# Hybrid RWKV-7 and dilated-attention layer: the second head's operands of the recurrent chain shifted by one 64-block, its diagonal results kept by one VectorE operation

## The chip, the cores and the metric

The kernel runs on one core of one Trainium2 chip. The metric is the device time of one execution in microseconds, the median of three runs for the kernel before. The engines are named as in the profile: PE is TensorE's matmul, PEld its weight load, DVE is VectorE, ACT is ScalarE, POOL is GpSimd, SP issues most transfers. Each engine works its instructions off in the order in which the program lists them, and waits at the first one that isn't ready.

## The reference, cut to what matters

One decoder layer on x of shape (1, 1024, 1024) in float32. An RMSNorm and one input projection give the inputs of two branches: 16 heads of RWKV-7 time mixing and 16 heads of dilated window attention. Both are gated and projected out together, with a final RMSNorm. The change lies in the time mixing, whose core is a recurrence over 1024 tokens with a 64 by 64 state per head:

```
def step(state, inp):
    r_t, w_t, k_t, v_t, av_t, bv_t = inp
    sa = jnp.einsum('bhvk,bhk->bhv', state, av_t)
    state = (state * w_t[:, :, None, :] + sa[..., None] * bv_t[:, :, None, :]
             + v_t[..., None] * k_t[:, :, None, :])
    return state, jnp.einsum('bhvk,bhk->bhv', state, r_t)
xs = (r_h, w_h, k_h, v_h, -kk, kk * a_h)   # w_h = exp(-exp(w)), kk a normalised key
_, y = lax.scan(step, s0, xs)
```

## The kernel before, in words

The time mixing is computed in chunks of 64 tokens. A unit is two heads (a pair, on partitions 0 to 63 and 64 to 127) and one half of the sequence, that is 8 chunks; 8 pairs by 2 halves give 16 units, worked off one after the other. While one unit is in the recurrent chain, the next is being inverted (`late`, `invert`), the one after that prepared (`prepare`, `products`), and the one before finished (`finish`). The loop in `rwkv` (line 346 on) writes these into 24 slots per unit, and after each slot takes some matmuls of the input projection from a generator (`advance`, line 363; L179 in the profile, each 128x512). They are there for PE to work on while the chain waits. The final order on each engine is set by the framework's scheduler, which reorders what is written by its own estimates of costs; so the order changes in many places when a few operations change.

The chain (`chain`, line 684) has three steps per chunk, each a matmul whose result goes from PSUM through one "spread" back to SBUF, where the next matmul takes it as its moving operand:

- `first`: z from the state Sd and the operand array AR (z<-Sd), spread into zd; and into T the products with Vd and Sd (T<-Vd, T<-Sd).
- `second`: z from zd and the inverse U (z<-zd), spread with the scale rn into ud.
- `third`: T from ud and TU (T<-ud), spread with the decay dec into the next Sd. The next chunk's z<-Vd follows.

The two heads are computed in one matmul. zd, ud and Sd are block diagonal, [128, 2, 64], with zeros in the off-diagonal blocks; the heads' results come out on partitions 0 to 63, one head in columns 0 to 63, the other in 64 to 127. `spread` therefore moves head 0's 64x64 block on DVE (L704 for zd, L707 for ud and Sd) and head 1's on ACT (L705, L708), which also changes its partitions:

```
if scale is None:
    V.tensor_copy(out=out[er[0], 0], in_=q[0:64, 0:64])
    S.copy(out=out[er[1], 1], in_=q[0:64, 64:128])
else:
    V.tensor_scalar(out=out[er[0], 0], in0=q[0:64, 0:64], scalar1=scale[0], ...)
    S.activation(out=out[er[1], 1], in_=q[0:64, 64:128], func=AF.Copy, scale=scale[1])
```

Other lines that are named below: L413 forms the log decays lw, L422 sums them, L438 and L170 are ACT work of the preparation and of the projection's weights, L483 is the receptance written into AR, L569 and L570 copy and mask products into MV, L604 and L606 are the columns of the inversion (two small DVE operations each), L627 and L655 transpose U, L216 is the token shift on DVE. After the time mixing (from about 840 us) come the attention and the output projection, which the change doesn't touch.

Of the kernel before, what the change touches and what calls it, by code (L numbers as in the profile page):

```python
# [24 lines left out]
C = 64  # L25
# [20 lines left out]
class Kern:  # L46
# [237 lines left out]
    def rwkv(self, pairs=range(NPAIR), apairs=range(NPAIR)):  # L284
        nc = self.nc
        with ExitStack() as ctx:
# [21 lines left out]
            for a in self.ARs:  # L308
                nc.gpsimd.memset(a[:, NC_ * 192:], 0.0)
                a = self.c192(a)  # L310
                for e in range(2):
                    er = slice(e * 64, e * 64 + 64)
                    nc.gpsimd.tensor_copy(out=a[er, :, 0], in_=bc(self.ident[er, er].unsqueeze(1), (64, NC_, 64)))
            self.d0 = pers.tile([128, 2, C + 1], F32, name="d0")
# [71 lines left out]
    def prepare(self, d):  # L386
# [78 lines left out]

# [28 lines left out]
    def late(self, d):  # L494
# [28 lines left out]
        def keys2(c4):  # L523
            tq, cs = t["tq"], slice(c4 * 4, c4 * 4 + 4)
            for e in range(2):
                er = slice(e * 64, e * 64 + 64)
                S.copy(out=d["TU"][er, cs, 0], in_=tq[0:64, :, e])
                S.copy(out=self.c192(d["MV"])[er, cs, 0], in_=tq[64:128, :, e])

# [13 lines left out]
    def products(self, d):  # L543
        nc = self.nc
        V, S, G = nc.vector, nc.scalar, nc.gpsimd
        er = [slice(0, 64), slice(64, 128)]

        def step(c4):
            AR, BK = d["AR"], d["BK"]
            if c4 == 0:  # L550
                d["TU"] = self.lng.tile([128, NC_, 3, 64], F32, name="TU")
                d["MV"] = self.lng.tile([128, NC_ * 192 + 2], F32, name="MV")
                G.memset(d["MV"][:, NC_ * 192:], 0.0)
            cs = slice(c4 * 4, c4 * 4 + 4)
            q = [self.ps_a.tile([128, 4, 128], F32, name=f"pa{e}") for e in range(2)]
            for b in range(4):
                c = c4 * 4 + b
                for e in range(2):
                    nc.tensor.matmul(q[e][:, b], lhsT=BK[er[e], c], rhs=AR[er[e], c * 192 + 64:c * 192 + 192], start=True,  # L559
                                     stop=True)  # L560
            d["pq"] = q

        def step2(c4):
            cs, q = slice(c4 * 4, c4 * 4 + 4), d["pq"]
            for e in (1, 0):
                V.tensor_tensor(out=d["TU"][er[e], cs, 1:3].rearrange("p c a t -> p c (a t)"), in0=q[e][0:64],
                                in1=bc(self.mask[0:64, 1].unsqueeze(1), (64, 4, 128)), op=ALU.mult)
                f = self.c192(d["MV"])[er[e], cs, 1:3].rearrange("p c a t -> p c (a t)")
# [21 lines left out]
    def invert(self, d, U):  # L590
# [17 lines left out]
        def clear():  # L608
            G.memset(U[:, 0:NC_], 0.0)

        def back():
            ud = self.dpool.tile([4, 16, 16, 16], F32, name="ud")
            nc.sync.dma_start(out=ud.rearrange("b q s t -> (b q) (s t)"), in_=d["UB"])
            for e in range(2):
                for b in range(4):
                    r = e * 64 + b * 16
                    nc.sync.dma_start(out=U[r:r + 16, 0:NC_, b * 16:b * 16 + 16],
                                      in_=ud[b, 8 * e:8 * e + 8].rearrange("q s t -> s q t"))
# [5 lines left out]
        def m0():  # L624
            t["UT"] = self.tmp("vr2", "UT", (128, NC_, C))
            t["Xs"] = self.inv.tile([128, NC_, 32], F32, name="Xs")
            V.transpose(out=fl(t["UT"]), in_=fl(U[:, 0:NC_]))  # L627

        def m1():
            xq = t["xq"] = self.ps_tr.tile([128, NC_, 16], F32, name="xq", tag="tr")  # L630
            for c in range(NC_):
                for g in range(4):
                    b = 32 * (g % 2)
                    nc.tensor.matmul(xq[hs(g), c], lhsT=t["LT"][rs(g), c, b:b + 16], rhs=U[rs(g), c, b + 16:b + 32], start=True,
                                     stop=True, skip_group_check=True)
# [5 lines left out]
        def m2():  # L641
            dq = t["dq"] = self.ps_tr.tile([128, NC_, 16], F32, name="dq", tag="tr")
            for c in range(NC_):
                for g in range(4):
                    b = 32 * (g % 2)
                    nc.tensor.matmul(dq[hs(g), c], lhsT=t["UT"][hs(g), c, b:b + 16], rhs=t["Xs"][hs(g), c, 0:16], start=True,
                                     stop=True, skip_group_check=True)

        def m2c():
            for g in range(4):  # L650
                b = 32 * (g % 2)
                S.copy(out=U[hs(g), 0:NC_, b + 16:b + 32], in_=t["dq"][hs(g)])
# [87 lines left out]
    def heads_out(self, d, c4):  # L740
# [423 lines left out]
```

## Time and profile before

| what | value |
|---|---|
| median of 3 runs | 1553.68 us (1553.39 to 1553.86) |
| profiled execution's own time | 1555.3 us |
| its span, first to last instruction | 1553.6 us |
| busy share of the span: PE, PEld, DVE, ACT, POOL | 96%, 77%, 65%, 58%, 28% |
| mean granted TensorE clock | 0.998 of full speed |
| chain that ended last, by engine | PE 60%, DVE 17%, ACT 16%, issue 3%, DMA 2%, POOL 1% |

A busy PE is not a PE at its peak, since its matmuls overlap and their ends are modelled. What a change on another engine can be worth to a kernel like this is read from where PE waits, and for what.

### The profile page before, as it was taken

How to read it: one execution, taken by the hardware profiler on the slowest of the kernel's cores; microseconds unless marked ns; L12 is line 12 of the kernel's file. 1: busy time of each engine (PE TensorE's matmuls, PEld its weight loads, DVE VectorE, ACT ScalarE, POOL GpSimd, SP SyncE). 2: the span in 40 equal slices, each digit the busy share in tenths (PEclk: the TensorE clock that was granted, in tenths of full speed). 3: DMA queues.
4: the chain of work that ended last, by engine and by line, in shares of the span. 5: the costliest groups of instructions: out<-in, count | busy, mean ns of one | idle time of the engine just before them, and what ended most of it. 6: DMA issues, size and time to landing. Idle time of an engine off the chain costs nothing.

```text
span 1553.6 us, 29135 instructions
## 1 busy us (share of the span) xinstructions
PE 1486.1 (96%) x10721; PEld 1201.3 (77%) x10721; DVE 1009.3 (65%) x2776; ACT 897.6 (58%) x2080; POOL 442.0 (28%) x563
## 2 busy tenths in 40 slices
PE   5999999999999999999999999999999999899997
PEld 4877777777777777777777788888888888787886
DVE  6866776667776677766743557667676666956144
ACT  6655666666676666666643556555565565655221
POOL 3211111111111121112211534334443343456442
PEclk9999999999999999999999999999999999999999
DMA  6321111111111111111111201111111111426452
GB/s 199 90 48 33 41 40 39 41 34 40 47 32 41 47 33 41 39 38 41 34 39 34 70 28 42 35 35 34 38 52 34 36 55 55 159 92 203 142 161 99
DMA packets 178829, 94.87 MB, mean 61 GB/s; under 512 B 58413, under 2 KB 164606, under 8 KB 178686
## 3 DMA queue, kind: packets, MB, share of 16 engines
q1 hardware_dynamic: 174942, 86.19, 19.4%
q10 hardware_dynamic: 3744, 6.82, 1.3%
q8 instruction: 84, 1.38, 0.4%
q14 instruction: 59, 0.48, 0.1%
HBM read 75.01 MB, written 17.83 MB: 60 GB/s over the span
## 4 chain that ended last, share of the span: by engine, by line
PE 60%; DVE 17%; ACT 16%; issue 3%; DMA 2%; POOL 1%; SPq 0%; DVEq 0%; ACTq 0%; POOLq 0%
PE pq L179 28%; PE oq L1048 10%; PE o L994 3%; PE z L693 3%; PE T L693 3%; PE mp L921 2%; PE sp L954 2%; ACT Y L745 1%; DVE I L422 1%; ACT MV L569 1%; PE sp L974 1%; ACT Vd L513 1%; DVE TB L604 1%; ACT shtmp L213 1%; PE pa L559 1%
## 5 line engine op out<-in xcount | busy, mean ns | idle before, releaser
L179 PE MATMUL pq<-xh,wh 128*128 128x512 f32 x1040 | 429.1, 413 | 0.0
L179 PE MATMUL pq<-xl,wh 128*128 128x512 f32 x1040 | 412.3, 396 | 0.0
L179 PE MATMUL pq<-xh,wl 128*128 128x512 f32 x1040 | 303.3, 409 | 0.0
L179 PEld LDWEIGHTS pq<-xh,wh 128*128 128x128 f32 x1040 | 195.9, 188 | 32.6 <-ACT xh L157 0.3
L179 PEld LDWEIGHTS pq<-xl,wh 128*128 128x128 f32 x1040 | 196.4, 189 | 30.9 <-DVE xl L158 0.4
L179 PEld LDWEIGHTS pq<-xh,wl 128*128 128x128 f32 x1040 | 184.5, 189 | 31.9
L1048 PE MATMUL oq<-ow,qr 128*128 128x512 f32 x512 | 161.9, 394 | 1.2 <-ACT ow L1029 0.6
L982 POOL TENSOR_TENSOR pl<-p,ph 128x512 fp32r<-128x512 f32 (+2 forms) x96 | 102.3, 1072 | 202.2 <-ACT ph L981 182.4
L923 DVE CUSTOM_DVE_ANT_0 mp<-mp,maskq 128x512 f32<-128x512 f32 (+1 forms) x192 | 105.5, 570 | 68.4 <-PE mp L921 59.9
L977 ACT ACTIVATE p<-p 128x512 f32<-128x512 f32 (+2 forms) x144 | 64.6, 452 | 104.2 <-DVE p L976 103.3
L171 POOL TENSOR_TENSOR wl<-wraw,wh 128x512 fp32r<-128x512 f32 x64 | 85.5, 1354 | 110.4 <-PE pq L179 58.4
L1043 POOL TENSOR_TENSOR vr<-kr,qr 128x512 fp32r<-128x512 f32 (+2 forms) x68 | 90.8, 1340 | 80.5 <-ACT qr L1042 70.0
L1048 PEld LDWEIGHTS oq<-ow,qr 128*128 128x128 f32 x512 | 95.9, 188 | 22.8 <-ACT ow L1029 1.1
L1048 PE MATMUL oq<-ow,vr 128*128 128x512 f32 x256 | 101.2, 395 | 1.9 <-POOL vr L1043 1.9
L170 ACT CAST wh<-wraw 128x512 fp32r<-128x512 f32 x138 | 80.7, 616 | 28.6 <-PE pq L179 23.4
L1042 ACT CAST qr<-kr 128x512 fp32r<-128x512 f32 (+2 forms) x68 | 40.2, 594 | 93.5 <-PE oq L1048 52.0
L976 DVE TENSOR_TENSOR p<-sp,maskt 128x512 f32<-128x512 f32 (+2 forms) x144 | 65.2, 457 | 43.3 <-PE sp L974 41.9
L570 POOL TENSOR_SCALAR_AFFINE_SELECT MV<-MV 64x512 f32<-64x512 f32 x64 | 47.8, 747 | 125.2 <-ACT MV L569 114.2
L708 ACT ACTIVATE ud<-z,rn 64x64 f32<-64x64 f32 x128 | 39.3, 307 | 65.3 <-DVE ud L707 63.6
L707 DVE TENSOR_SCALAR ud<-z,rn 64x64 f32<-64x64 f32 x128 | 34.3, 268 | 58.1 <-PE z L693 57.9
L693 PEld LDWEIGHTS T<-ud,TU 128*128 128x128 f32 x256 | 42.5, 188 | 34.8 <-ACT ud L708 28.2
L708 ACT ACTIVATE Sd<-T,dec 64x64 f32<-64x64 f32 x120 | 36.9, 307 | 53.5 <-DVE Sd L707 52.0
(236 smaller groups left out, 3158.4 us busy)
## 6 DMA issues: line engine op xcount, KB each, us to landing
wraw<-in_w_in_dram SPq DMA_DIRECT2D x138, 256.0 KB
kr<-mixd SPq DMA_DIRECT2D x60, 256.0 KB
oraw<-in_w_out_dram SPq DMA_DIRECT2D x16, 512.0 KB
xt<-in_x_dram SPq DMA_DIRECT2D x8, 512.0 KB
ld<-TU SPq DMA_DIRECT2D x32, 128.0 KB
mixd<-zt SPq DMA_DIRECT2D x16, 256.0 KB
mixd<-gt SPq DMA_DIRECT2D x16, 256.0 KB
xr<-in_x_dram ACTq DMA_DIRECT2D x16, 256.0 KB
```

Source lines behind the costliest of these rows:

```text
L170: nc.scalar.copy(out=wh[:, ks], in_=raw)
L171: eng.tensor_tensor(out=wl[:, ks], in0=raw, in1=wh[:, ks].bitcast(F32), op=ALU.subtract)
L179: return [lambda i=i, a=a, b=b: self.nc.tensor.matmul(q, lhsT=a, rhs=b, start=(i == 0), stop=(i == len(ops) - 1)) for i, (a, b) in enumera ...
L570: G.affine_select(out=f, in_=f, pattern=[[0, 4], [-1, 2], [1, 64]], compare_op=ALU.is_ge, fill=0.0, base=0, channel_multiplier=-1)
L693: mm = lambda out, w, x, start, stop: nc.tensor.matmul(out, lhsT=w, rhs=f2(x), start=start, stop=stop, skip_group_check=True)
L708: S.activation(out=out[er[1], 1], in_=q[0:64, 64:128], func=AF.Copy, scale=scale[1])
L923: V.tensor_tensor_reduce(out=mp[:, :kn], in0=mp[:, :kn], in1=self.maskq[:, v0:v0 + kn], op0=ALU.add, op1=ALU.max, scale=1.0, scalar=-3e38, ...
L976: V.tensor_tensor(out=p[:, :qn], in0=sp[:, :qn], in1=self.maskt[:, u0:u0 + qn], op=ALU.add)
L977: S.activation(out=p[:, :qn], in_=p[:, :qn], func=AF.Exp)
L982: G.tensor_tensor(out=pl[:, :qn], in0=p[:, :qn], in1=ph[:, :qn].bitcast(F32), op=ALU.subtract)
L1043: nc.gpsimd.tensor_tensor(out=ml, in0=raw, in1=mh.bitcast(F32), op=ALU.subtract)
L1048: nc.tensor.matmul(q, lhsT=m[:, i], rhs=v, start=(k == 0 and j == 0), stop=(k == 15 and j == 2))
```

## The change

Head 1's operands are laid one 64-block later than head 0's, so that the matmuls put head 0's result on partitions 0 to 63 and head 1's on 64 to 127, where the spread needs it. A full 128x128 result then has the wanted blocks on its diagonal, and unwanted products off it. For ud and Sd one scalar_tensor_tensor on DVE scales the whole 128x128 and multiplies it with the constant block mask `bd`; ACT has no part in it. For zd the result is not shifted (both heads on partitions 0 to 63), and both halves are copied by DVE. Along with this:

- the operands AR, TU, MV and U change their layout: the identity block, receptance and masks go to other blocks for head 1 (`ra`), U's head 1 starts one block later, and `second` loads 128 columns of U as weights instead of 66;
- the receptance (L483) becomes two operations of 64 partitions, the mask on POOL (L570) two operations of half the size, the transposes of U and its clearing 576 columns instead of 512;
- the log decays move from DVE to ACT; the small ACT copies rn1 and dec's second half go.

```
 def logs():
-    V.tensor_scalar(out=lw[:, :, 0:C], in0=c3(th), scalar1=-DECAY / 2, scalar2=-DECAY / 2,
-                    op0=ALU.mult, op1=ALU.add)
+    S.activation(out=lw[:, :, 0:C], in_=c3(th), func=AF.Copy, scale=-DECAY / 2, bias=-DECAY / 2)
...
 def decrease():
-    d["dec"] = self.mid.tile([64, 2, NC_], F32, name="dec", bufs=3)
-    G.tensor_copy(out=d["dec"][:, 0], in_=Ux[0:64, :, 0])
-    S.copy(out=d["dec"][:, 1], in_=Ux[64:128, :, 0])
+    d["dec"] = self.mid.tile([128, NC_], F32, name="dec", bufs=3)
+    G.tensor_copy(out=d["dec"], in_=Ux[:, :, 0])
...
-    d["rn1"] = self.mid.tile([64, NC_], F32, name="rn1", bufs=3)
-    S.copy(out=d["rn1"], in_=rn[64:128])
...
 def receptance():
-    V.tensor_tensor(out=self.c192(d["AR"])[:, :, 1], in0=c3(d["rs"]), in1=d["W"][:, :, 1:C + 1], op=ALU.mult)
+    for e in range(2):
+        er = slice(e * 64, e * 64 + 64)
+        V.tensor_tensor(out=self.c192(d["AR"])[er, :, 1 - e], in0=c3(d["rs"])[er], in1=d["W"][er, :, 1:C + 1],
+                        op=ALU.mult)
...
 def step2(c4):
-        S.copy(out=f, in_=q[e][64:128])
-        G.affine_select(out=f, in_=f, pattern=[[0, 4], [-1, 2], [1, 64]], compare_op=ALU.is_ge, fill=0.0, base=0,
-                        channel_multiplier=-1)
+        S.copy(out=f, in_=cat(q[e][64:128]))
+        for j in range(2):
+            G.affine_select(out=f[:, :, j], in_=f[:, :, j], pattern=[[0, 4], [1, 64]], compare_op=ALU.is_ge, fill=0.0,
+                            base=-j, channel_multiplier=-1)
...
 def m0():
-    V.transpose(out=fl(t["UT"]), in_=fl(U[:, 0:NC_]))
+    V.transpose(out=fl(t["UT"]), in_=fl(U))
...
 def spread(out, q, scale):
-    if scale is None:
-        V.tensor_copy(out=out[er[0], 0], in_=q[0:64, 0:64])
-        S.copy(out=out[er[1], 1], in_=q[0:64, 64:128])
-    else:
-        V.tensor_scalar(out=out[er[0], 0], in0=q[0:64, 0:64], scalar1=scale[0], scalar2=None, op0=ALU.mult)
-        S.activation(out=out[er[1], 1], in_=q[0:64, 64:128], func=AF.Copy, scale=scale[1])
+    V.scalar_tensor_tensor(out=f2(out), in0=q, scalar=scale, in1=self.bd, op0=ALU.mult, op1=ALU.mult)
...
 def first(c):
-    spread(zd, t["z"][:, 0], None)
+    V.tensor_copy(out=zd[er[0], 0], in_=t["z"][0:64, 0, 0:64])
+    V.tensor_copy(out=zd[er[1], 1], in_=t["z"][0:64, 0, 64:128])
...
 def second(c):
-    mm(t["z"][0:66, 1], f2(d["U"])[:, c * 64:c * 64 + 66], self.zds[c % 2], True, True)
-    spread(self.uds[c % 2], t["z"][:, 1], [d["rn"][0:64, c:c + 1], d["rn1"][:, c:c + 1]])
+    mm(t["z"][:, 1], f2(d["U"])[:, c * 64:c * 64 + 128], self.zds[c % 2], True, True)
+    spread(self.uds[c % 2], t["z"][:, 1], d["rn"][:, c:c + 1])
...
 def third(c):
-    spread(self.Sds[(c + 1) % 2], T, [dec[:, e, n:n + 1] for e in range(2)])
+    spread(self.Sds[(c + 1) % 2], T, dec[:, n:n + 1])
```

The order on the engines moves with it. The place shown is the second chunk of the unit that runs at 510 us in the trace of before, around the spread into ud. In these rows zd, ud and Sd are the chain's spreads, TB and UB the inversion's columns, AR, BK and ks the preparation, bv, rs and wl other work. DVE before:

```order
L704 COPY zd_127<-z 64x64
L606 TENSOR_TENSOR UB<-UB,TB 64x12x4
L469 SCALAR_TENSOR_TENSOR AR_143<-ks,prm,W 128x8x64
L604 TENSOR_TENSOR TB<-UB,AB 64x39
L472 SCALAR_TENSOR_TENSOR BK<-ta,Ux 128x8x64
L606 TENSOR_TENSOR UB<-UB,TB 64x13x3
L476 SCALAR_TENSOR_TENSOR BK<-ks,prm,BK 128x8x64
L604 TENSOR_TENSOR TB<-UB,AB 64x28
L707 TENSOR_SCALAR ud_129<-z,rn 64x64
```

DVE now, at the same place:

```order
L717 COPY zd_127<-z 64x64
L607 TENSOR_TENSOR TB<-UB,AB 64x48
L718 COPY zd_127<-z 64x64
L609 TENSOR_TENSOR UB<-UB,TB 64x12x4
L421 SCALAR_TENSOR_TENSOR I<-d_154,lw 128x130
L607 TENSOR_TENSOR TB<-UB,AB 64x39
L609 TENSOR_TENSOR UB<-UB,TB 64x13x3
L607 TENSOR_TENSOR TB<-UB,AB 64x28
L609 TENSOR_TENSOR UB<-UB,TB 64x14x2
L607 TENSOR_TENSOR TB<-UB,AB 64x15
L609 TENSOR_TENSOR UB<-UB,TB 64x15
L707 SCALAR_TENSOR_TENSOR ud_129<-z,rn,bd 128x128
```

The three long operations of the preparation (AR, BK, BK) no longer stand between zd and ud; they come after ud. The two copies into zd have another operation between them, as 47 of the 128 such pairs have.

ACT before, from the preparation's L438 on (a), with the two casts of weights (wh) around the spread into ud:

```order
L438 ACTIVATE a<-ta,hk 128x512
L170 CAST wh<-wraw 128x512
L708 ACTIVATE ud_129<-z,rn_4899 64x64
L170 CAST wh<-wraw 128x512
L708 ACTIVATE Sd_122<-T_5937,dec 64x64
L213 ACTIVATE shtmp<-pq,prm 128x512
L705 COPY zd_126<-z 64x64
L708 ACTIVATE ud_128<-z,rn_4899 64x64
```

ACT now, at the same place:

```order
L432 ACTIVATE Ux<-I 128x520
L170 CAST wh<-wraw 128x512
L436 ACTIVATE a<-ta,hk 128x512
L170 CAST wh<-wraw 128x512
L213 ACTIVATE shtmp<-pq,prm 128x512
L745 COPY Y<-T_5833 64x256 x2
```

The spreads are gone from ACT, and nothing of the chain stands behind its long operations.

PE before, from z<-zd to the next chunk's z<-Sd (pq is the projection, bq the bonus product):

```order
L693 MATMUL z<-zd_127,U_118 66x128
L179 MATMUL pq<-xh_79,wl 128x512 x4
L533 MATMUL bq<-bh,bdr 128x512
L533 MATMUL bq<-bl,bdr 128x512
L179 MATMUL pq<-xh_79,wl 128x512 x2
L693 MATMUL T_5937<-ud_129,TU 128x128
L693 MATMUL z<-Vd_120,MV 66x128
L179 MATMUL pq<-xh_79,wl 128x512 x2
L693 MATMUL T_6206<-Vd_120,MV 128x128
L179 MATMUL pq<-xh_78,wh 128x512
L693 MATMUL z<-Sd_122,AR_144 66x128
```

PE now, over the same steps:

```order
L697 MATMUL z<-zd_127,U_118 128x128
L179 MATMUL pq<-xh_79,wl 128x512 x4
L697 MATMUL T_5833<-ud_129,TU 128x128
L697 MATMUL z<-Vd_120,MV 66x128
L532 MATMUL bq<-bh,bdr 128x512
L532 MATMUL bq<-bl,bdr 128x512
L179 MATMUL pq<-xh_79,wl 128x512 x4
L697 MATMUL z<-Sd_122,AR_144 66x128
```

Between z<-zd and T<-ud stood eight wide matmuls, now four; the other four moved behind T<-ud, where six now stand ahead of z<-Sd instead of three.

## Rows read from the trace of the kernel before

**Rows 1.** Windows: the time-mixing stretch; busy us and (instructions) of each engine, clock, DMA.

```profile
80.00:840.00 760.00, 729.76 (x7042) 567.62 (x7041) 514.26 (x1676) 476.87 (x1239) 124.91 (x242) 1.00 0.16 39
```

**Rows 2.** Waits of PE: who waited for whom; us in total, times, longest.

```profile
PE T L693 <- ACT ud L708: 8.9, 15, 1.3
PE z L693 <- ACT zd L705: 4.8, 15, 0.5
PE bq L533 <- ACT Vd L513: 4.5, 8, 1.5
PE z L693 <- ACT Sd L708: 3.8, 19, 0.5
```

**Rows 3.** Waits of PE's weight loads, same columns.

```profile
PEld T L693 <- ACT ud L708: 28.2, 56, 1.8
PEld z L693 <- ACT Sd L708: 24.3, 48, 0.9
PEld z L693 <- ACT zd L705: 14.8, 26, 0.9
```

**Rows 4.** Groups by line and shape, the chain on PE: count, busy us, mean ns, idle before.

```profile
L693 PE MATMUL T<-ud,TU 128*128 128x128 f32 x256 | 55.4, 298 | 10.0 <-ACT ud L708 8.9
L693 PE MATMUL z<-Sd,AR 128*66 128x128 f32 x256 | 51.4, 282 | 4.8 <-ACT Sd L708 3.8
L693 PE MATMUL z<-zd,U 128*66 128x128 f32 x256 | 50.4, 278 | 4.9 <-ACT zd L705 4.8
L693 PE MATMUL T<-Vd,MV 128*128 128x128 f32 x256 | 49.6, 275 | 0.0
...
L693 PE MATMUL z<-Vd,MV 128*66 128x128 f32 x256 | 49.0, 273 | 0.0
...
L693 PEld LDWEIGHTS T<-ud,TU 128*128 128x128 f32 x256 | 42.5, 188 | 34.8 <-ACT ud L708 28.2
...
L693 PEld LDWEIGHTS z<-zd,U 128*66 128x66 f32 x256 | 32.5, 137 | 27.8 <-ACT zd L705 14.8
```

**Rows 5.** Timeline of PE at 508.5 us: start, us, instruction, [idle before].

```profile
508.60 0.38 PE L693 MATMUL z<-zd,U 128*66 128x128 f32 x2
...
511.94 0.49 PE L693 MATMUL T<-ud,TU 128*128 128x128 f32 x2 [0.69 <-ACT ud L708]
```

**Rows 6.** Timeline of DVE at the same place.

```profile
510.13 0.27 DVE L707 TENSOR_SCALAR ud<-z,rn 64x64 f32<-64x64 f32 x1
```

**Rows 7.** Timeline of ACT at the same place.

```profile
510.23 0.82 ACT L438 ACTIVATE a<-ta,hk 128x512 f32<-128x512 f32 x1
510.95 0.60 ACT L170 CAST wh<-wraw 128x512 fp32r<-128x512 f32 x1
511.58 0.31 ACT L708 ACTIVATE ud<-z,rn 64x64 f32<-64x64 f32 x1
```

**Rows 8.** Groups by line and shape: DVE operations that price the new ones.

```profile
L707 DVE TENSOR_SCALAR ud<-z,rn 64x64 f32<-64x64 f32 x128 | 34.3, 268 | 58.1 <-PE z L693 57.9
...
L704 DVE COPY zd<-z 64x64 f32<-64x64 f32 x128 | 27.0, 211 | 40.5 <-PE z L693 38.7
...
L976 DVE TENSOR_TENSOR p<-sp,maskt 128x512 f32<-128x512 f32 x32 | 22.0, 688 | 31.4 <-PE sp L974 31.4
...
L976 DVE TENSOR_TENSOR p<-sp,maskt 128x128 f32<-128x128 f32 x48 | 13.1, 274 | 6.6 <-PE sp L974 5.5 <-POOL pl L982 0.9
...
L216 DVE SCALAR_TENSOR_TENSOR rs<-pq,om,shtmp 128x512 f32<-128x512 f32 x16 | 12.0, 750 | 0.7
```

**Rows 9.** Groups by line on DVE between 200 and 700 us: the log decays.

```profile
L413 DVE TENSOR_SCALAR lw<-th 128x512 f32<-128x512 f32 x11 | 4.7, 425 | 0.6
```

**Rows 10.** Windows: 5 us in the unit's first half, columns as in rows 1.

```profile
499.00:504.00 5.00, 4.51 (x29) 3.63 (x28) 4.83 (x18) 3.08 (x10) 0.53 (x2) 1.00 0.00 0
```

**Rows 11.** Groups by line and shape: the mask on POOL.

```profile
L570 POOL TENSOR_SCALAR_AFFINE_SELECT MV<-MV 64x512 f32<-64x512 f32 x64 | 47.8, 747 | 125.2 <-ACT MV L569 114.2 <-DVE vs L216 5.0 <-DVE ks L216 4.0
```

**Rows 12.** Waits of DVE for POOL.

```profile
DVE vs L216 <- POOL MV L570: 5.7, 7, 0.9
```

More of the change, by code (lines that the diff above doesn't have):

```diff
@@ L312, in rwkv @@
                     er = slice(e * 64, e * 64 + 64)
-                    nc.gpsimd.tensor_copy(out=a[er, :, 0], in_=bc(self.ident[er, er].unsqueeze(1), (64, NC_, 64)))
+                    nc.gpsimd.tensor_copy(out=a[er, :, e], in_=bc(self.ident[er, er].unsqueeze(1), (64, NC_, 64)))
             self.d0 = pers.tile([128, 2, C + 1], F32, name="d0")
@@ L526, in keys2 @@
                 er = slice(e * 64, e * 64 + 64)
-                S.copy(out=d["TU"][er, cs, 0], in_=tq[0:64, :, e])
-                S.copy(out=self.c192(d["MV"])[er, cs, 0], in_=tq[64:128, :, e])
+                S.copy(out=d["TU"][er, cs, e], in_=tq[0:64, :, e])
+                S.copy(out=self.c192(d["MV"])[er, cs, e], in_=tq[64:128, :, e])
         def bonus():
@@ L546, in products @@
         er = [slice(0, 64), slice(64, 128)]
+        ra = [slice(1, 3), slice(0, 3, 2)]
+        at = lambda ap: ap.rearrange("p (a t) -> p a t", a=2)
+        cat = lambda ap: ap.rearrange("p c (a t) -> p c a t", a=2)
         def step(c4):
@@ L558, in step @@
                 for e in range(2):
-                    nc.tensor.matmul(q[e][:, b], lhsT=BK[er[e], c], rhs=AR[er[e], c * 192 + 64:c * 192 + 192], start=True,
+                    nc.tensor.matmul(at(q[e][:, b]), lhsT=BK[er[e], c], rhs=self.c192(AR)[er[e], c, ra[e]], start=True,
                                      stop=True)
@@ L565, in step2 @@
             for e in (1, 0):
-                V.tensor_tensor(out=d["TU"][er[e], cs, 1:3].rearrange("p c a t -> p c (a t)"), in0=q[e][0:64],
-                                in1=bc(self.mask[0:64, 1].unsqueeze(1), (64, 4, 128)), op=ALU.mult)
-                f = self.c192(d["MV"])[er[e], cs, 1:3].rearrange("p c a t -> p c (a t)")
-                S.copy(out=f, in_=q[e][64:128])
-                G.affine_select(out=f, in_=f, pattern=[[0, 4], [-1, 2], [1, 64]], compare_op=ALU.is_ge, fill=0.0, base=0,
-                                channel_multiplier=-1)
+                V.tensor_tensor(out=d["TU"][er[e], cs, ra[e]], in0=cat(q[e][0:64]),
+                                in1=cat(bc(self.mask[0:64, 1].unsqueeze(1), (64, 4, 128))), op=ALU.mult)
+                f = self.c192(d["MV"])[er[e], cs, ra[e]]
+                S.copy(out=f, in_=cat(q[e][64:128]))
+                for j in range(2):
+                    G.affine_select(out=f[:, :, j], in_=f[:, :, j], pattern=[[0, 4], [1, 64]], compare_op=ALU.is_ge, fill=0.0,
+                                    base=-j, channel_multiplier=-1)
         def relayout():
@@ L608, in clear @@
         def clear():
-            G.memset(U[:, 0:NC_], 0.0)
+            G.memset(U, 0.0)
         def back():
@@ L616, in back @@
                     r = e * 64 + b * 16
-                    nc.sync.dma_start(out=U[r:r + 16, 0:NC_, b * 16:b * 16 + 16],
+                    nc.sync.dma_start(out=U[r:r + 16, e:NC_ + e, b * 16:b * 16 + 16],
                                       in_=ud[b, 8 * e:8 * e + 8].rearrange("q s t -> s q t"))
@@ L624, in m0 @@
         def m0():
-            t["UT"] = self.tmp("vr2", "UT", (128, NC_, C))
+            t["UT"] = self.tmp("vr2", "UT", (128, NC_ + 1, C))
             t["Xs"] = self.inv.tile([128, NC_, 32], F32, name="Xs")
-            V.transpose(out=fl(t["UT"]), in_=fl(U[:, 0:NC_]))
+            V.transpose(out=fl(t["UT"]), in_=fl(U))
         def m1():
@@ L633, in m1 @@
                     b = 32 * (g % 2)
-                    nc.tensor.matmul(xq[hs(g), c], lhsT=t["LT"][rs(g), c, b:b + 16], rhs=U[rs(g), c, b + 16:b + 32], start=True,
+                    nc.tensor.matmul(xq[hs(g), c], lhsT=t["LT"][rs(g), c, b:b + 16], rhs=U[rs(g), c + g // 2, b + 16:b + 32], start=True,
                                      stop=True, skip_group_check=True)
@@ L645, in m2 @@
                     b = 32 * (g % 2)
-                    nc.tensor.matmul(dq[hs(g), c], lhsT=t["UT"][hs(g), c, b:b + 16], rhs=t["Xs"][hs(g), c, 0:16], start=True,
+                    nc.tensor.matmul(dq[hs(g), c], lhsT=t["UT"][hs(g), c + g // 2, b:b + 16], rhs=t["Xs"][hs(g), c, 0:16], start=True,
                                      stop=True, skip_group_check=True)
@@ L651, in m2c @@
                 b = 32 * (g % 2)
-                S.copy(out=U[hs(g), 0:NC_, b + 16:b + 32], in_=t["dq"][hs(g)])
+                S.copy(out=U[hs(g), g // 2:NC_ + g // 2, b + 16:b + 32], in_=t["dq"][hs(g)])
         def m2t():
-            V.transpose(out=fl(t["UT"]), in_=fl(U[:, 0:NC_]))
+            V.transpose(out=fl(t["UT"]), in_=fl(U))
         lo = [slice(e * 64, e * 64 + 32) for e in range(2)]
@@ L662, in m3 @@
                 for e in range(2):
-                    nc.tensor.matmul(x2[hi[e], c], lhsT=d["TU"][lo[e], c, 2, 32:64], rhs=t["UT"][lo[e], c, 0:32], start=True,
+                    nc.tensor.matmul(x2[hi[e], c], lhsT=d["TU"][lo[e], c, 2, 32:64], rhs=t["UT"][lo[e], c + e, 0:32], start=True,
                                      stop=True, skip_group_check=True)
@@ L673, in m4 @@
                 for e in range(2):
-                    nc.tensor.matmul(x2[lo[e], c], lhsT=t["Xs"][hi[e], c], rhs=U[hi[e], c, 32:64], start=True, stop=True,
+                    nc.tensor.matmul(x2[lo[e], c], lhsT=t["Xs"][hi[e], c], rhs=U[hi[e], c + e, 32:64], start=True, stop=True,
                                      skip_group_check=True)
@@ L678, in m4c @@
             for e in range(2):
-                S.copy(out=U[lo[e], 0:NC_, 32:64], in_=t["x2"][lo[e]])
+                S.copy(out=U[lo[e], e:NC_ + e, 32:64], in_=t["x2"][lo[e]])
         return [(COLS[j], lambda j=j: column(j)) for j in range(15)] + [
@@ L744, in heads_out @@
         for e in range(2):
-            self.nc.scalar.copy(out=d["Y"][e * 64:e * 64 + 64, 4 * c4:4 * c4 + 4], in_=d["T", c4][64:128, :, e * 64:e * 64 + 64])
+            self.nc.scalar.copy(out=d["Y"][e * 64:e * 64 + 64, 4 * c4:4 * c4 + 4], in_=d["T", c4][64 - e * 64:128 - e * 64, :, e * 64:e * 64 + 64])
     def finish(self, d):
```

## The prediction

> **What bounds the kernel now.** I read the stretches first, then who waits for whom, then one place in order of time. In the time-mixing stretch, 80 to 840 us, PE is busy 729.76 of 760.00 us and DVE and ACT 514.26 and 476.87 [rows 1]. PE sets the time, and what a change on DVE and ACT can give back is PE's idle time there, 760.00 - 729.76 = 30.2 us, and whatever hides in stretched matmuls. The list of PE's waits says whose it is: the three links of the chain, each ended by ACT's half of a spread, make 8.9 + 4.8 + 3.8 = 17.5 us in 49 waits (15, 15 and 19), and one non-chain wait for ACT another 4.5 us [rows 2]. The reader is to see that DVE is named in none of the four: ACT's half is always the later one, because it starts only after DVE's. The weight loads wait longer, 28.2 + 24.3 + 14.8 = 67.3 us [rows 3], much of it while the matmul in front still runs, so that is an upper bound. Some of it is seen in the matmuls: those that follow a spread average 298, 282 and 278 ns, where the same shape with ready operands takes 275 or 273 [rows 4]. Over 256 each that is 256 x 23, 9 and 5 ns = 5.9 + 2.3 + 1.3 = 9.5 us. The chain's visible stalls are thus 17.5 + 9.5 = 27.0 us.
>
> One stall in order of time shows what a link is made of. z<-zd ends at 508.60 + 0.38 = 508.98; DVE begins its half of ud at 510.13, so it was 1.15 us late, and ends at 510.40; ACT begins its half at 511.58, 1.18 us later, behind the long operations a and wh, and ends at 511.89; T<-ud starts at 511.94, after 0.69 us of idle PE [rows 5 to 7]. Of 2.96 us, queueing and work on DVE are 1.42 and on ACT 1.49.
>
> **The change part by part.**
>
> *The spreads.* One operation takes the place of two in series for ud and Sd. No row shows a scalar_tensor_tensor of 128x128 from PSUM. A tensor_tensor of that shape and source takes 274 ns, and at 512 columns the scalar form takes 750 against 688 [rows 8], so I take 274 + 62 = 336 ns; its ends are 274 and 750. A link for ud or Sd then costs the DVE queue plus 0.34 us. At the place above: 1.15 + 0.34 + 0.05 for the hand-over as before = 1.54 instead of 2.96 us. But the cover shrinks too: there PE had eight wide matmuls and 2.96 - 0.69 = 2.27 us of work over this link, and in the new order four, some 1.14 us. The stall would fall from 0.69 to about 0.40, not to nothing, since the order is packed to what its planner expects. For zd the DVE work doubles (2 x 211 ns instead of 211 and an ACT copy), and 47 of the 128 pairs have another operation between them; here only ACT's queue is gained. What else can be late is DVE's queue. So I take 60% of the 27.0 us as gained, **-16.2 us**, between nothing and the 67.3 of the loads.
>
> *ACT relieved.* 128 + 128 + 120 spreads leave ACT, and 16 log decays of between 0.60 and 0.82 us each (the two 128x512 operations of rows 7) come to it. The Vd copies behind which PE waits 4.5 us [rows 2] should come earlier: half of it, **-2.2 us**, between 0 and 4.5.
>
> *DVE loaded.* ud and Sd: 248 x (336 - 268) ns = 16.9 us, with Sd priced as ud. The second zd copy: 128 x 211 = 27.0. The second receptance: 16 x 688 = 11.0, since a half of the partitions with 512 columns is priced by its columns. Two transposes per unit over 64 columns more: the slope from 128 to 512 columns is (688 - 274)/384 = 1.08 ns [rows 8], so 32 x 69 ns = 2.2. The log decays go: 16 x 425 = -6.8 [rows 9]. The sum is 50.3 us, and DVE goes from 514.26 to 564.6 of 760 us, 68% to 74%. It is covered by PE's matmuls unless a link is late. So far 27.0 us of visible stall stand against 514.26 + 476.87 = 991 us of DVE and ACT work, 2.7%; at that rate 50.3 us show up as **+1.3 us**. If the cover is gone it is all 50.3, which is the second rival's matter.
>
> [...]
>
> *Wider weights.* `second` loads 128 columns of U instead of 66. With ready operands the two widths give matmuls of 275 and 273 ns [rows 4]: 256 x 2 ns = **+0.5 us**. Where a load is waited for, its own 188 instead of 137 ns are in the open: at most 256 x 51 ns = 13.1 us.
>
> *POOL.* The mask becomes two operations, each between half of 747 ns and all of it [rows 11], so 0 to 47.8 us more on an engine that is busy 124.91 of 760 us [rows 1]. What is queued behind it is the first column of the token shift, for which DVE waits 7 times, 5.7 us in all [rows 12]. Each could be later by half an operation, 7 x 0.37 = 2.6 us of DVE idle; at the rate above nothing of it reaches PE: 0, at most 2.6. The small ACT copies that go and the wider clearing of U are no part of any link: 0.
>
> *Moved work.* AR, BK and BK now come after ud. Their reader is PE's products, late in the unit. With 68% on average and far more in the first half [rows 10], DVE has room there; I count 0, and leave it to the second rival if that room is gone.
>
> *Sum.* -16.2 - 2.2 + 1.3 + 0.5 = -16.6 us. The profiled execution took 1555.3 us (span 1553.6, 1.7 around it), so 1538.7. The median of the runs is 1.6 us lower, 1553.7, and so the forecast is **1537 us**.
>
> **The rivals.**
>
> *The stall only changes its name.* DVE's queue takes ACT's place: with twice the copies for zd and less cover at ud, links end as late as before. For it: at 510 us DVE alone was 1.15 us late, and PE's cover is cut from eight to four there. Against it: DVE is named in none of PE's chain waits, and AR, BK and BK have left the link. Gain 0 to 5 us: about 1552.
>
> *DVE becomes the bound in the first half of a unit (slower).* At 499 to 504 us DVE is busy 4.83 of 5.00 us [rows 10], 0.17 free. Per chunk the change adds 211 + 2 x 68 = 347 ns, and 5 us hold nearly one chunk (eight in a unit of some 47 us, 760/16). Such dense stretches are some 20 us of a unit, so 1.2 us come to each against 0.7 us of room. If all of it falls on the links, 16 x 1.2 = 19 us are lost, and only half of the 16.2 + 2.2 us, 9 us, is gained: 1554 + 10 = 1564. It decides from the point where DVE's work between two links is longer than PE's cover, that is as soon as 0.35 us more don't fit into 0.17. Against it: the order puts off the long operations, and on average DVE has room.
>
> [...]
>
> *More than the visible stall goes.* The loads' 67.3 us are lost time in larger part than I count. At the same 60% it is 40 us: about 1513.
>
> **How the numbers follow.** Forecast 0.54; its own range runs from all of 27.0 + 4.5 gained (less 1.8: 1524) to a third of the 27.0 and no relief (-9 + 1.8: 1547). Changed name 0.18, slower 0.16, more 0.12. What a measurement of this kernel can tell from no change is about 0.2%, 3 us, so 1550.6 to 1556.8 counts as the same. Of the changed name a third ends below that; faster is 0.54 + 0.12 + 0.06 = 0.72, the same 0.12, slower 0.16. The range for 8 in 10 takes in the third rival's point and the first's, and part of the way to the second's: 1513 to 1558.
>
> **What the changed profile would show.** Right: ACT gone from PE's chain waits, those for DVE below 10 us in sum, T<-ud's mean below 285 ns, the new ud and Sd near 336 ns, DVE near 565 us busy in the stretch and the stretch shorter by 15 to 20 us. The changed name would show as 15 us or more of PE waits on DVE's ud. The slower case would show DVE above 4.95 of 5 us in the first half of a unit, and PE waiting for zd or AR. The forecast is wrong as well if the new operation takes 450 ns or more, or if z<-zd with its wider weights lengthens by 30 ns or more.

## The result: 1526.8 us, faster, and by more than forecast

The changed kernel takes 1526.83 us (median of 4 runs, 1524.43 to 1529.3) where the kernel before took 1553.77 beside it: a ratio of 0.9825, 95% interval 0.9805 to 0.9845. The gain is 26.9 us; the forecast had 16.6. The profiled execution took 1524.43 us, its span is 1522.7. It is the fastest of its four, and the profiled one of before is the slowest of its four, so that the two profiles below lie 30.9 us apart and not 26.9.

The page's busy times of the kernel after:

```profile
PE 1466.4 (96%) x10721; PEld 1210.9 (80%) x10721; DVE 1061.1 (70%) x2904; ACT 794.0 (52%) x1688; POOL 446.9 (29%) x627
```

Before, PE was busy 1486.1 of 1553.6 us. The span is 30.9 us shorter, and that is 19.7 us of busy PE and 11.2 us of idle PE (67.5 became 56.3). So the larger part is not in any list of waits. Nearly all of it lies in the time mixing, whose last T<-ud starts at 813.58 us where it started at 843.38. DVE works 51.8 us more (1009.3 before; the prediction had 50.3), ACT 103.6 us less (897.6 before).

The shares of the chain that ended last, after:

```profile
PE 71%; DVE 18%; ACT 5%; issue 4%; DMA 1%; POOL 0%; DVEq 0%; SPq 0%; ACTq 0%; POOLq 0%
```

Before, PE had 60% of it and ACT 16%. ACT's share has fallen to 5%, and DVE's went only from 17% to 18%.

Who PE waits for, after (us in total, times, longest):

```profile
PE yq L778 <- DVE Y L772: 8.1, 14, 1.7
PE T L697 <- DVE ud L707: 4.8, 8, 0.6
...
PE pa L561 <- DVE BK L476: 2.3, 2, 1.4
...
PE z L697 <- DVE zd L718: 2.1, 4, 1.5
```

Against [rows 2] the reader sees the chain's 17.5 us in 49 waits become 6.9 in 12, all for DVE; Sd is gone, and the bonus product's 4.5 us for ACT have shrunk to 0.2. Two names are new or grown: the transposes of the finished Y (`yq`, 1.4 us before) and the products of AR and BK (`pa`), both waiting for DVE's side work and not for a spread.

The weight loads' waits, after, against the 67.3 us of [rows 3]:

```profile
PEld T L697 <- DVE ud L707: 19.9, 42, 1.1
PEld z L697 <- DVE zd L718: 14.0, 33, 1.9
PEld yq L778 <- DVE Y L772: 13.6, 16, 2.1
...
PEld z L697 <- DVE Sd L707: 2.5, 8, 0.5
```

The chain's part is now 36.4 us. The groups by line and shape that answer to [rows 4] and [rows 8], after (count, busy us, mean ns, idle before):

```profile
L697 PE MATMUL T<-ud,TU 128*128 128x128 f32 x256 | 53.8, 292 | 5.8 <-DVE ud L707 4.8
L697 PE MATMUL z<-zd,U 128*128 128x128 f32 x256 | 52.6, 287 | 2.5 <-DVE zd L718 2.1
L697 PE MATMUL z<-Sd,AR 128*66 128x128 f32 x256 | 49.0, 273 | 0.0
L707 DVE SCALAR_TENSOR_TENSOR ud<-z,rn,bd 128x128 f32<-128x128 f32 x128 | 43.0, 336 | 35.5 <-PE z L697 35.5
L707 DVE SCALAR_TENSOR_TENSOR Sd<-T,dec,bd 128x128 f32<-128x128 f32 x120 | 41.7, 347 | 26.5 <-PE T L697 24.8
...
L637 PE MATMUL xq<-U,LT 32*16 32x16 f32 x1024 | 13.9, 175 | 0.0
```

The new operation costs 336 and 347 ns where 336 was forecast. The last row is one to stop at. Before, it was

```profile
L634 PE MATMUL xq<-U,LT 32*16 32x16 f32 x1024 | 19.8, 175 | 1.3 <-DMA U<-ud 1.2
```

The 1024 small matmuls of `xq` take 175 ns each in both kernels, and the time that they cover fell from 19.8 to 13.9 us. Their number and duration didn't change, only how many pieces they are cut into. PE's timeline shows it, first before, then after:

```profile
518.07 0.21 PE L634 MATMUL xq<-U,LT 32*16 32x16 f32 x2
519.30 0.21 PE L634 MATMUL xq<-U,LT 32*16 32x16 f32 x2
520.56 0.21 PE L634 MATMUL xq<-U,LT 32*16 32x16 f32 x2
522.18 0.64 PE L634 MATMUL xq<-U,LT 32*16 32x16 f32 x58
```

```profile
503.01 0.69 PE L637 MATMUL xq<-U,LT 32*16 32x16 f32 x64
```

The same 64 matmuls cover 1.27 us in four pieces and 0.69 in one. The ends overlap what follows; from the start of each piece to the start of the next matmul it is 0.98 us (three times 0.14, and 0.56) against 0.61. Over the whole trace xq stands in 62 pieces before and 32 after, `pa` in 61 and 45. So PE's order is a suspect beside the spreads.

### The profile page after: what moved, and what is told of

Its sections match the earlier page's. It is cut to its first block, busy times and chain, and to the rows that moved or that the text cites. A ratio compares the mean times of both kernels' runs of the same rounds, so it can differ in the third digit from the quotient of the medians.

```text
span 1522.7 us, 28998 instructions
## 1 busy us (share of the span) xinstructions
PE 1466.4 (96%) x10721; PEld 1210.9 (80%) x10721; DVE 1061.1 (70%) x2904; ACT 794.0 (52%) x1688; POOL 446.9 (29%) x627
## 4 chain that ended last, share of the span: by engine, by line
PE 71%; DVE 18%; ACT 5%; issue 4%; DMA 1%; POOL 0%; DVEq 0%; SPq 0%; ACTq 0%; POOLq 0%
PE pq L179 35%; PE oq L1048 10%; PE T L697 4%; PE z L697 4%; PE o L994 3%; PE pa L561 2%; PE mp L921 2%; DVE TB L607 2%; DVE UB L609 2%; PE sp L954 2%; DVE I L421 1%; PE sp L974 1%; PE sp L973 1%; DVE ow L1030 1%; PE xq L637 1%
## 5 line engine op out<-in xcount | busy, mean ns | idle before, releaser
L179 PE MATMUL pq<-xh,wl 128*128 128x512 f32 x1040 | 295.2, 405 | 0.0
L573 POOL TENSOR_SCALAR_AFFINE_SELECT MV<-MV 64x256 f32<-64x256 f32 x128 | 58.1, 476 | 50.7 <-ACT MV L571 49.0
L745 ACT COPY Y<-T 64x256 f32<-64x256 f32 x64 | 23.4, 366 | 88.1 <-PE xq L637 80.0
L707 DVE SCALAR_TENSOR_TENSOR ud<-z,rn,bd 128x128 f32<-128x128 f32 x128 | 43.0, 336 | 35.5 <-PE z L697 35.5
L697 PEld LDWEIGHTS z<-zd,U 128*128 128x128 f32 x256 | 44.9, 188 | 22.6 <-DVE zd L718 14.0
```

The lines of the kernel that those rows point to most:

```text
L179: return [lambda i=i, a=a, b=b: self.nc.tensor.matmul(q, lhsT=a, rhs=b, start=(i == 0), stop=(i == len(ops) - 1)) for i, (a, b) in enumera ...
L573: G.affine_select(out=f[:, :, j], in_=f[:, :, j], pattern=[[0, 4], [1, 64]], compare_op=ALU.is_ge, fill=0.0, base=-j, channel_multiplier=-1)
L697: mm = lambda out, w, x, start, stop: nc.tensor.matmul(out, lhsT=w, rhs=f2(x), start=start, stop=stop, skip_group_check=True)
```

## The experiments

Theory: the gain comes from the shorter link. Rival: it comes from the new order on PE. To part them PE's order is held by order-only edges between neighbouring matmuls, which make nothing wait for another engine. DVE's and ACT's orders are still made by the scheduler around it. The runs fall into three groups, with medians of before of 1555.1 (the table below and the halves on DVE and ACT), 1553.86 and 1554.87; a difference of medians across groups is uncertain by about these 1.2 us, and the ratios take that out.

**The changed kernel in the old order of PE, the old kernel in the new order, and a control** (the changed kernel held in its own order). The edit is the same in the three, with another list; that of the first is (names shortened)

```
+    mm = [i for i in nc.cur_bb.bb.instructions if type(i).__name__ == "InstMatmult"]
+    for a, b in zip(order, order[1:]):        # order: PE's in the kernel before
+        tc.add_manual_dep(mm[b], mm[a].name, DependencyInfo(NoSync, DATA), reason="pin")
```

> The changed kernel with all its PE instructions held in the order of the kernel before (only the order is held, no wait is added). Theory A, the shorter spread is what gives the time: about 1527 us, at most 4 above the changed kernel, since the spreads are as in the changed kernel. Theory B, the order gives a good part (the small matmuls xq and pa stand in 130 groups before and 84 after): 1536 to 1542, with 10 us or more lost to changes between kinds of matmul although PE's waits for the chain stay as small as in the changed kernel.

> The kernel before with all its PE instructions held in the order of the changed kernel. Theory A: 1554 us or more, since the spreads are the old ones and some covers are shorter (four wide matmuls instead of eight between z<-zd and T<-ud). Theory B: 1540 to 1546, since the order's share comes without the spreads.

> Control: the changed kernel with its PE instructions held in its own order. Both theories: the same instructions in the same order on every engine, so the changed kernel's 1527 us within 3 us.

Measured (PE busy and idle are of the profiled execution):

| spreads | PE's order | median us | ratio to before (95%) | PE busy | PE idle |
|---|---|---|---|---|---|
| old | old (before) | 1555.1 | 1 | 1486.1 | 67.5 |
| new | old | 1555.57 | 1.0004 (0.9995 to 1.0013) | 1475.5 | 79.1 |
| old | new | 1571.53 | 1.0108 (1.0092 to 1.0123) | 1475.5 | 90.9 |
| new | new, held | 1525.6 | 0.981 (0.9797 to 0.9824) | 1467.2 | 56.3 |

Neither alone gains anything. The new operations in the old order are worth nothing, the new order with the old operations costs 16 us, and both together give 29.5. By the theory the first of these was to stay at 1527 us, and by the rival to come to 1536 to 1542; it lost the whole gain. The busy column nearly adds up: 10.6 us less by either, 18.9 by both. The idle column doesn't: each alone adds idle time, both together take it away.

One reading has to go with the medians, here and below: the TensorE clock that was granted. In these traces it stands at one of two levels, full speed or half of it (1.00 and 0.50 in the clock column of the windows). Summed over windows of 1 us, PE stood at the lower level for 6.0 us before, for 7.6 and 7.4 in the second and the last row of the table, and for 17.1 in the third. The clock is halved there, so at most half of the 11 us more is lost time: of the 16 us that the third row is above before, up to some 6 can be the clock's.

Where the idle time goes is in PE's waits, first of the new spreads in the old order:

```profile
PE yq L778 <- DVE Y L772: 20.1, 14, 1.8
...
PE bq L532 <- ACT Vd L512: 10.8, 13, 1.2
PE pa L561 <- DVE BK L476: 4.1, 2, 2.6
...
PE z L697 <- DVE zd L718: 2.0, 6, 0.3
...
PE T L697 <- DVE ud L707: 1.3, 2, 0.7
```

The chain's waits are cured, 3.3 us for 17.5. But yq went from 1.4 to 20.1 us and bq from 4.5 to 10.8: 14 and 13 waits, about one a unit, of at most 1.8 and 1.2 us. What stands in front, on DVE and then on PE, in the same kernel:

```profile
499.45 0.68 DVE L454 TENSOR_REDUCE nq<-sqt 128x8 f32<-128x512 f32 x1
...
500.78 0.34 DVE L707 SCALAR_TENSOR_TENSOR Sd<-T,dec,bd 128x128 f32<-128x128 f32 x1
...
501.60 0.69 DVE L772 TENSOR_TENSOR Y<-Y,gr 128x512 f32<-128x512 f32 x1
```

```profile
502.35 0.66 PE L778 MATMUL yq<-ident,Y 128*128 128x128 f32 x4 [1.78 <-DVE Y L772]
```

PE sits 1.78 us for the scaling of Y, which DVE starts at 501.60 after a norm's reduction and a spread. The reading is that DVE, which works in order (in the changed kernel's trace its 2904 operations start in the order of the program), has the result late, and that the place of its reader in PE's order was made for an earlier result; the next run and the last one try it. Now the old kernel in the new order:

```profile
PE T L693 <- ACT ud L708: 31.7, 33, 1.9
...
PE zq L400 <- ACT zt L786: 5.1, 13, 0.5
```

And its row of xq has the busy time of the changed kernel (14.0 against 13.9 us; the wait for a transfer in front of it is a single one), so the pieces come with the order alone:

```profile
L634 PE MATMUL xq<-U,LT 32*16 32x16 f32 x1024 | 14.0, 175 | 4.8 <-DMA U<-ud 4.8
```

With less cover over the link (eight wide matmuls between z<-zd and T<-ud in the orders shown ahead, now four), the ACT half of ud is in the open: 31.7 us for 8.9 before. Only the short link makes up for the short cover.

**Only yq and bq moved.** The changed kernel in before's order of PE, but with these two kinds of matmul where the new order has them. The edit is the list again; it was put together like this (in short):

```
+    if kind(k) in ("yq", "bq"): after_of[previous in the new order].append(k)
+    for k in order_before_without_them: c.append(k); c += after_of.get(k, [])
```

> The changed kernel with PE held in the order of the kernel before, except that the transposes yq and the bonus products bq stand where the changed kernel has them. Theory C, DVE's later results meet matmuls that stand too early (yq 20.1 and bq 10.8 us of PE's waits with the old order): both waits fall to about 10 us together, and the time from 1555.6 to 1531 to 1536; what stays above the changed kernel is the 9 us of PE busy time. Theory D, the old order loses by its 46 more groups of small matmuls: at most 8 us are gained, 1548 or more.

It took 1544.4 us, ratio 0.9939 (0.9926 to 0.9951), between what the two theories had: 11.2 of the 30 us between the two orders come back by these two kinds, so they are not the whole of what the order is worth. In its waits bq is down to 0.6 us and yq still large:

```profile
PE yq L778 <- DVE Y L772: 12.3, 14, 2.0
...
PE pa L561 <- DVE BK L476: 4.1, 2, 2.6
PE z L697 <- DVE zd L718: 3.6, 7, 0.6
```

Its span is still 16.9 us above the control's, and 11.3 of these are busy time, 1478.5 us against 1467.2. At most 5.5 of them can be the clock's (18.4 us at the lower level against 7.4); the rest is put down to the small pieces, which stand here as in the old order, and the next run tries that.

**The pieces gathered.** The changed kernel in its own order, with each unit's xq and pa in fewer pieces (48 for 77). The list was made like this (in short):

```
+    if k in g: held[g[k]].append(k)           # g: the xq or pa group of a matmul
+        if last[g[k]] == i: out += held.pop(g[k])
+    else: out.append(k)
```

> The changed kernel with PE held in its own order, but the small matmuls xq and pa of a step gathered where the last of them stood (groups of them on PE from 77 to 48 in the time mixing). Theory D (each group costs PE about 9.1/46 = 0.2 us): 6 us faster than the changed kernel, about 1520. Theory C alone: within 3 us of it.

It took 1521.55 us, 0.9795 (0.9781 to 0.9808). The control's ratio is 0.981, so this is about 2 us better by the ratios and 4.1 by the medians, with intervals that overlap. xq's row goes on falling:

```profile
L637 PE MATMUL xq<-U,LT 32*16 32x16 f32 x1024 | 11.0, 175 | 0.0
```

PE is busy 1459.3 us, 7.9 less than in the control: 0.27 us for each of 29 pieces, of which 2 to 4 us show as time (up to 4.8 more may be hidden by the clock, 16.9 us at the lower level against 7.4). The change itself took away 46 pieces; at this price 12.5 us, near the 10.6 us of busy time that the new order alone saves. That is an estimate and not a separation: the new order also has fewer and longer runs of the projection's xh,wl matmuls, whose row falls by 7.2 us (303.3 to 296.1) with the order alone.

**The hop to ACT brought back, in the new order.** The halves of ud and Sd again on DVE and ACT, PE held:

```
-        V.scalar_tensor_tensor(out=f2(out), in0=q, scalar=scale, in1=self.bd, op0=ALU.mult, op1=ALU.mult)
+        V.tensor_scalar(out=out[er[0], 0], in0=q[0:64, 0:64], scalar1=scale[0:64], ...)
+        S.activation(out=out[er[1], 1], in_=q[64:128, 64:128], func=AF.Copy, scale=scale[64:128])
```

> The changed kernel, PE held in its own order, with the spreads into ud and Sd done in two halves again: head 0's block on DVE, head 1's on ACT, from the shifted layout. Theory A: most of the gain in the links of ud and Sd goes, 10 to 15 us are lost, 1537 to 1542, and PE's waits name ACT at ud and Sd. Theory B: at most 5 us lost, 1527 to 1532.

It took 1567.86 us, 1.0084 (1.007 to 1.0098): in this order the one operation is worth 42 us, far more than either theory had.

```profile
PE T L697 <- ACT ud L708: 31.1, 44, 2.0
...
PE z L697 <- ACT Sd L708: 2.6, 9, 0.8
```

Not all of the 42 us are waits. Here is PE in one of the dense places, and the window after the long wait (columns as in [rows 1]):

```profile
226.77 1.18 PE L179 MATMUL pq<-xh,wl 128*128 128x512 f32 x4
229.88 0.49 PE L697 MATMUL T<-ud,TU 128*128 128x128 f32 x2 [1.94 <-ACT ud L708]
...
231.43 1.91 PE L179 MATMUL pq<-xh,wl 128*128 128x512 f32 x4
```

```profile
230.00:234.00 4.00, 4.00 (x17) 3.32 (x17) 1.76 (x4) 1.87 (x4) 0.42 (x2) 0.57 0.16 25
```

PE stands idle for 1.94 us, and then the clock falls to 0.50 for 3.4 us, in which four matmuls of the projection take 1.91 us instead of 1.18. The same happens at four more places, after waits of 1.95 to 1.97 us; after one of 1.96 us, the one that ends at 421.63, the clock stays up. Over the whole run PE stands at the lower level for 35.3 us (6.8 of them ahead of the chain, at 18 to 26 us), against 7.4 in the control. So up to 14 of the 42 us are the clock's, and not the waits' themselves.

**Two halves, both on DVE.** As the one before, with both halves `V.tensor_scalar`; no hop, but one more instruction in the link.

> The changed kernel, PE held in its own order, with the spreads into ud and Sd as two operations of 64x64, both on DVE: 248 x (2 x 268 - 336) ns = 50 us more on DVE and a link 0.2 us longer, but no hop to ACT. If the hop to ACT's queue is what the halves on two engines lose (1567.9): 1537 to 1550, waits on DVE's ud and yq. If one operation instead of two is what counts: 1560 or more.

It took 1571.61 us, 1.0123 (1.0107 to 1.0138). Its clock is near the control's (9.5 us at the lower level against 7.4).

```profile
PE T L697 <- DVE ud L708: 22.7, 45, 1.0
PE yq L779 <- DVE Y L773: 12.5, 14, 1.7
...
PE z L697 <- DVE Sd L708: 6.1, 15, 0.9
```

DVE is busy 1132.5 us, 72.5 more than in the control (50 were expected), and the kernel 46.0 us slower: 63% of what is added to DVE shows, most of it added inside the chain's links. So taking the hop between engines away gives nothing back; with two operations in series the link is late on either engine. How much of the 46 us is the longer link and how much the load on DVE, these two runs can't part; the run before, late with DVE at 1045.5 us, shows that the load isn't needed for it.

**The second zd copy on ACT.** 

```
-            V.tensor_copy(out=zd[er[1], 1], in_=t["z"][0:64, 0, 64:128])
+            S.copy(out=zd[er[1], 1], in_=t["z"][0:64, 0, 64:128])
```

> The changed kernel, PE held in its own order, with the second copy into zd back on ACT: 27 us less on DVE. Theory C: PE's wait for yq falls from 8.1 us to below 4, that for zd grows by 2 to 8 us with ACT named: 1523 to 1531. Theory A, any hop to ACT costs the link as it does at ud (31 us of waits there): 1540 or more.

It took 1532.61 us, 0.9866 (0.9851 to 0.9881), 7.0 slower than the control by the medians (9 by the ratios), with PE no busier (1464.6).

```profile
PE T L697 <- DVE ud L707: 8.6, 15, 1.0
PE z L697 <- ACT zd L718: 5.2, 12, 1.0
PE zq L400 <- ACT zt L786: 4.1, 13, 0.4
...
PE yq L778 <- DVE Y L772: 1.7, 1, 1.7
```

This is the trade in one list. DVE, 28 us lighter (1032.1), has Y in time, and yq falls from 8.0 to 1.7; the zd link now ends on ACT, and the lateness goes down the chain to ud and zq. The copy on DVE is right, by little.

**The log decays back on DVE.**

```
-            S.activation(out=lw[:, :, 0:C], in_=c3(th), func=AF.Copy, scale=-DECAY / 2, bias=-DECAY / 2)
+            V.tensor_scalar(out=lw[:, :, 0:C], in0=c3(th), scalar1=-DECAY / 2, scalar2=-DECAY / 2, ...)
```

> The changed kernel, PE held in its own order, with the log decays back on DVE: 16 x 425 ns = 6.8 us more on DVE, 16 x 628 ns = 10 us less on ACT. If DVE's load is nearly all in the open, as the 50 us of the two DVE halves were (46 us lost): 5 to 7 us slower, about 1531. At the prediction's 2.7%: no change, 1525.6 within 2 us.

It took 1537.24 us, 0.9887 (0.9869 to 0.9905), 11.6 slower than the control, for some 7 us of work on DVE.

```profile
PE yq L779 <- DVE Y L773: 8.1, 14, 1.7
PE xq L638 <- DMA U<-ud: 4.8, 4, 3.6
...
PE bq L533 <- ACT Vd L513: 2.0, 2, 1.7
```

Its six runs scatter over 10 us (1532.7 to 1542.72), the control's four over 1.4 and the other kernels' over at most 7.5. The clock goes with it: the three slowest runs (1538.33, 1541.64 and 1542.72 us) have a mean granted clock of 0.988 or 0.989, the three others 0.991 to 0.994, the control 0.996 to 0.999. Ahead of one of the falls PE had stood idle: 3.6 us for a transfer, a wait that the control doesn't have; then came 13.7 us at the lower level (two neighbouring windows, columns as in [rows 1]):

```profile
104.00:108.00 4.00, 0.80 (x7) 0.52 (x6) 0.00 (x0) 0.55 (x1) 1.69 (x3) 1.00 0.32 89
108.00:121.70 13.70, 13.30 (x169) 9.48 (x170) 5.08 (x8) 4.92 (x13) 2.08 (x6) 0.51 0.04 5
```

In the whole run it is 35.0 us against the control's 7.4, and up to 13.8 us lost by that, more than the 11.6 that are to be explained. So nothing is shown of what DVE's load costs here. Why the transfer is late stays open; that the move to ACT does no harm is all the run shows.

**DVE's order improved.** On top of the gathered pieces: the 47 separated zd pairs made neighbours on DVE; and in a second kernel also the norms `nq` and `rn` behind the last scaling of Y. DVE's list was made like this (in short):

```
+        if k in first: out.append(o[first[k]])        # zd's second copy right behind the first
...
+        if inside and (f[0] in ("nq", "rn")): hold.append(x); continue    # put back behind Y<-Y,gr
```

> The gathered version (PE's small matmuls in 48 groups, 1521.6 us) with DVE held in its order too, except that in the 47 pairs of copies into zd that had another operation between them the second copy stands right behind the first. If the separation is a cost of the new zd: 17 operations of 0.75 us and 30 of 0.2 us leave the link, up to 19 us; where PE waits for zd (2.6 us, and 14 us of weight loads) 2 to 6 us are gained, 1516 to 1520. If the cover hides it: 1521.6 within 2 us.

> The same with one more move on DVE: the reduction nq and the scales rn of the unit being prepared, which nothing needs soon, stand behind the last scaling of Y instead of in front of it, so that Y is some 1.1 us earlier. If PE's wait for yq is DVE's order and nothing else: the wait falls from 8.1 us to about 1, and the time by another 6 to 8 us, 1510 to 1514. If Y waits for ACT's squares or the chain instead: no gain.

They took 1522.09 us, 0.9788 (0.9776 to 0.9801), and 1523.03, 0.9791 (0.9779 to 0.9804): no different from the gathered pieces alone. The waits of the second:

```profile
PE T L697 <- DVE ud L707: 11.6, 22, 0.7
PE z L697 <- DVE Sd L707: 3.6, 7, 0.8
...
PE yq L778 <- DVE Y L772: 2.3, 3, 1.7
```

yq lost 5.8 us, and ud and Sd took up 9.7 more than in the gathered kernel (4.9 and 0.6 there). So the wait for yq was DVE's order, as read above, but no time came of moving it: in these two tries the order on DVE only chose who is late.

The lowest median is that of the gathered pieces, 1521.55 us, clear of before and, by 5.3 us across groups, below the changed kernel; its interval and that of the changed kernel (0.9805 to 0.9845) touch, so that it is the faster of the two is likely, not shown.

## Why the prediction was right, and where it was off

Right was the mechanism and its side: PE's chain waits were ACT's, one operation on DVE takes them away, and ACT's share of the path falls from 16% to 5%. The forecast came out 10 us too high. That it came so near is in part luck: held in the old order of PE, the same terms gave nothing (1555.57 us), and what PE's order brought had no term at all. Of its signs, the chain's waits for DVE (6.9 us), the price of the operation and DVE's work came out as named; T<-ud's mean did not, and the time mixing got shorter by 30 us, not 15 to 20. By its own steps:

- **The spreads, -16.2.** Waits of the chain: 17.5 to 6.9, -10.6. The means of the three matmuls, against 275 and 273 ns with ready operands: 17, 12 and 0 ns over 256 each, 7.4 us for 9.5, -2.1. Together -12.7; in the old order, by its rows (T<-ud 283 ns, z<-zd 289, z<-Sd 273, 3.3 us of waits), -18.1. The term was sized well, and the reason for not taking all 27 was right: cover shrinks where the link does. T<-ud's 292 ns missed its 285, since part of the stall stayed. The price of the operation (336 and 347 ns for 336) held.
- **ACT relieved, -2.2.** bq's wait fell by 4.3, from 4.5 to 0.2, but only with its new place: in the old order it rose to 10.8.
- **DVE loaded, +1.3.** The work was right, 50.3 us forecast and 51.8 measured (a receptance half of 64x512 took 707 ns, the whole of 128x512 676 before); the rate of 2.7% was the mis-sized step. It averaged over the stretch, and the waits that came stand where DVE is dense (14 for yq, about one a unit; around one of them, at 482 to 487 us, DVE is busy 4.87 of 5.00 us). The new waits for DVE's side work are yq +6.7 and pa +2.3, 9.0 us, in the kernel's own order; 46.0 us for 72.5 is what a load in the links shows as.
- **Wider weights, +0.5.** z<-zd's mean went from 278 to 287 ns, a stall included; far from the 30 ns named. **POOL, 0:** no wait of PE for the mask came up. **Moved work, 0:** pa's 2.3 us of waits for BK are its price, small and already counted.
- **What had no term.** These measured sizes sum to about -7.5 us (-12.7 - 4.3 + 9.0 + 0.5), against 30.9 us of span. The 2 by 2 table shows what is missing: PE's order. PE's busy time falls by 10.6 us through the order alone, with the old spreads, with fewer pieces of xq and pa; and by another 10.6 through the new spreads alone, of which the three means show about 3 (-3.7, +2.8 and -2.3 us in the three groups). That second 10.6 us brought no time in the old order: idle PE grew by 11.6. The prediction read three places of the order, for covers, and let the diff of the rest pass as costless; counting the pieces of xq (62 to 32) before the run would have shown that there was something to price.

Of the rivals, *the stall only changes its name* describes the new spreads in the old order exactly, with another name than it said: 1555.57 us, the stall being at yq and not at ud. *DVE becomes the bound* has the right mechanism in yq and pa, and is nearest to what the two halves on DVE make of it, 1571.61. *More than the visible stall goes* (1513) is the rival nearest in time to the result, though farther off than the forecast: the chain's loads wait 30.9 us less, and 10.6 us of busy PE went with the spreads alone.

Not settled: which part of those 10.6 us is stall hidden in stretched matmuls or between them, which parts of PE's order beside yq, bq and the pieces carry the 30 us between the two orders, and how the new spreads would do in the old order of all engines; holding DVE as it stood before wasn't tried, since its instructions are not the same.

## What to carry to other kernels

An operation that shortens a link is worth what the order around it lets through: here nothing in the old order of PE, 42 us in the new, up to 14 of them by the clock. So compare the order on the bottleneck engine as a whole, count in how many pieces small operations are cut, and look where the readers of side results stand. A load on an engine that works in order, as DVE does here, is better priced in its densest stretch, at its critical time, than by its average share: here 9.0 us of new waits came where that share gave 1.3. And before the waits of a slower variant are made to explain its time, read for how long its clock was down.

## What the runs showed of the hardware

- 64 small matmuls cover 1.27 us of PE in four pieces between wide ones and 0.69 in one, 0.98 and 0.61 from start to next start; over 29 pieces, 0.27 us of busy PE each.
- A scalar_tensor_tensor of 128x128 from PSUM takes 336 to 347 ns; two tensor_scalars of 64x64 in a row on DVE take 265 and 291 (ud), 556 ns together. One full operation with a mask was cheaper than two quarter ones.
- In the kernel with ACT's halves, after PE had stood idle for 1.94 us, the granted clock fell to 0.50 of full speed for 3.4 us, and four wide matmuls took 1.91 us instead of 1.18. Over that run the stretches at 0.50 came to 35.3 us, in the control to 7.4.
- Moving 16 operations of less than 1 us (the log decays) gave runs that scatter over 10 us instead of 1.4; the slower ones are those with the lower mean clock (0.988 and 0.989 against 0.991 to 0.994).
